# First loads reordered and cut, two more tiles' latents from unscaled tokens, separate PSUM banks for a tile's second transposition

## The chip, the cores and the metric

The kernel runs on one core of one Trainium2 chip. The metric is the device time of one execution in microseconds, the median of several runs; lower is better. Beside the timed runs, one execution was recorded by the hardware profiler, and all views of the profile and the trace come from that one.

## The reference

One encoder layer for 1280 tokens of width 1024 (256 of a prompt, 1024 of a sample), all in float32:

```python
h = rmsnorm(x, attn_norm_g)
proj = h @ w_in                      # 384 q latent | 256 kv latent | 32 rope key | 3 x 512 neighbourhood q, k, v
a = mla_group(proj[..., :o1], proj[..., o1:o2], proj[..., o2:o3], q_norm_g, kv_norm_g, w_uq, w_ukv)
b = na_group(proj[..., o3:], na_rpb)
mix = jnp.concatenate([rmsnorm(a, mla_out_g), rmsnorm(b, na_out_g)], axis=-1)
x = x + mix @ w_o
h2 = rmsnorm(x, ffn_norm_g)
x = x + (jax.nn.silu(h2 @ w_gate) * (h2 @ w_up)) @ w_down
```

with a final `rmsnorm`. For this case only the head of it matters: the norm of the tokens, the first 672 columns of `proj` (the latents), the norms of the q and kv latents with their gains, the rotation of the rope key, and the rope part of the queries, which is computed from the normed q latent. A norm of a token is one scale per row, so `rmsnorm(x) @ w` can be taken as `(x @ w)` scaled per row afterwards.

## The kernel before, in words

The tokens are ten tiles of 128 (`NT`), the width eight chunks of 128 (`KC`). Every float32 product is made of three float32r matmuls (`mm3`, lines 108 to 112): each operand is held as a rounded high part and the remaining low part, and high x high, high x low and low x high accumulate in PSUM. So each operand costs a cast on ScalarE (high) and a subtraction on VectorE or GpSimd (low).

The part up to line 295 computes the latents. Its pieces:

- `load_wc(kc)` (line 138) loads one chunk of the latent weights, 128 x 672, and splits it with the norm's gain folded in (`split_g`). Chunks 0 to 4 land in buffers that later hold other weights, chunks 5 to 7 in a ring of two (`wc_raw`).
- `load_half` and `split_x` (lines 149 to 156) load a half of a transposed token tile and split it into `hT_h` and `hT_l`.
- `rms_x(t)` (line 158) loads the same tokens row by row, squares and sums them on ScalarE and makes the row's scale `r` on GpSimd.
- `scale_x(t)` (line 167) spreads `r` over a matrix on GpSimd (`r_m`), turns it on TensorE (`rr`), multiplies the transposed tile by it on VectorE and splits it again. `hT_h` and `hT_l` hold the scaled tokens from then on, for the q, k and V projections that follow.
- `norm_tile(t)` (line 176) is load, row scale and `scale_x` in one.
- `latents(t, r0)` (line 182) runs 48 matmuls into two accumulators (`lat`, four banks in turns of two: 384 columns for q, 288 for kv and the rope key), copies them out to `c`, norms both latents, rotates the key, and turns `c` on TensorE: four transpositions into one `trc` bank, then two more into the same one bank. With `r0` given, the tokens were not scaled yet and the copy out applies `r0`.
- `rope_q(t)` (line 241) makes the rope part of the queries in the bank `pr` (nine matmuls, a rotation, two transpositions) and stores it to `rope_d`.

Tiles 0 to 2 (`NU = 3`) have their latents taken from unscaled tokens and are scaled afterwards; tile 3 is scaled before the loop, and tiles 4 to 9 by `norm_tile(t + 3)` at the head of turn `t`. In the loop's turn `t` stand, in this order, that norm, `latents(t)`, `scale_x(t)` for the unscaled ones, and `rope_q(t)`.

Behind the loop come the weights of the neighbourhood q and k projection (`qk_weights`, line 300), V's weights and V's matmuls for all tiles (`wv_raw`, `wv_h`, `na_t`), and the q and k projections themselves (`qk_ftile`, line 310, accumulators `pj`). V's weights take the memory that the latent stage's pools (`ra`) free.

Order of the work: all loads go through one queue (SP) in the order in which the program writes them; a load that waits for its buffer holds up those behind it. Stores go through ScalarE's queue. The other engines' instruction orders are written by a planner, which runs the program through a model of times and takes what is ready, earlier lines first; on the chip each engine then follows its list strictly. `HOLD` (line 130) keeps four of the chunks of the q/k projections back until a named step of the latents: `(i, c0)` names weight block `i` and first token `c0`; `(t, 0)`, `(t, 1)` and `(t, 2)` are tile `t`'s first transposition, its second, and the one of its rope queries.

PSUM has eight banks: before the change four for `lat`, one `trc`, one `pr`, two `rr`; when `rr` is freed at turn 7, `pj` takes its two.

Of the kernel before, what the change touches and what calls it, by code (L numbers as in the profile page):

```python
# [39 lines left out]
def encoder_trunk(ctx: ExitStack, tc: tile.TileContext, x_tm, x_T, g_attn, w_c, w_v, w_qk,  # L40
# [97 lines left out]
    def load_wc(kc):  # L138
        nm = ("wqk_raw", "wqk_h", "wqk_l", "wqk_h", "wqk_l")
        raw = (rb.tile([P, KC, P], F32, name=nm[kc], bufs=1 if kc == 0 else 2)  # L140
               .rearrange("p a b -> p (a b)")[:, 0:CW] if kc < 5 else
               rx.tile([P, CW], F32, name="wc_raw", bufs=2))
# [4 lines left out]
        wc.append((h, l))

    def split_x(t, xT, q=None):
        ks = slice(0, KC) if q is None else slice(4 * q, 4 * q + 4)  # L150
# [1 line left out]
        nc.scalar.copy(out=hT_h[sl], in_=xT[:, ks])
        nc.vector.tensor_sub(out=hT_l[sl], in0=xT[:, ks], in1=hT_h[sl])
# [13 lines left out]
    def scale_x(t, xT, r):  # L167
        rm = ra.tile([P, P], F32, name="r_m", bufs=1)
        nc.gpsimd.tensor_scalar(out=rm, in0=ones, scalar1=r, scalar2=1.0, op0=ALU.mult,
                                op1=ALU.mult)  # L170
# [1 line left out]
        nc.tensor.matmul(rr, lhsT=rm, rhs=ident, start=True, stop=True)
# [1145 lines left out]
```

## Time and profile before

| | |
|---|---|
| median of 3 runs | 1643.68 us (1642.41 to 1643.81) |
| the profiled execution, own time | 1647.12 us |
| its span, first to last instruction | 1645.3 us |
| mean granted TensorE clock | 0.991 |
| TensorE busy | 1594.9 us, 97% of the span |
| VectorE busy | 884.6 us, 54% |
| ScalarE busy | 715.5 us, 43% |
| GpSimd busy | 660.4 us, 40% |
| first matmul | 6.68 us after the first instruction |
| first matmul of V | 157.05 us |

A row of the timeline has the start, the duration, the engine, the line, the operation, `out<-in` with the program's names, the shapes, how many were merged, and in brackets how long the engine had been idle before it and what released it. PE is TensorE's matmul, PEld its weight load, DVE VectorE, ACT ScalarE, POOL GpSimd, SP the engine whose queue issues the loads (its rows are marked SPq). Where a helper records an operation, the line is the helper's: L110 to L112 are the three matmuls of `mm3`, L99 and L100 the split of a PSUM bank, L64 every load.

### The profile page before, as it was taken

To read this page: it belongs to the slowest core of one execution; us is meant where nothing else is said; L and a number is where in the kernel's file an instruction comes from. 1 tells how busy PE (TensorE), PEld (TensorE's weight loads), DVE (VectorE), ACT (ScalarE), POOL (GpSimd) and SP (SyncE) were. 2 spreads that over 40 slices of the span, in tenths; PEclk is the share of its full clock that TensorE was granted. 3 is DMA by queue.
4 is the path that set the end of the run, shared out by engine and by line. 5 is a ranking of instruction groups with operands and counts; after the bars stand their busy time and mean duration, and the time that the engine had idled before them with its cause. 6 is when DMAs were issued, how large, how long until landed. Compare 5 with 4: busy or idle time off the path is not lost.

```text
span 1645.3 us, 25695 instructions
## 1 busy us (share of the span) xinstructions
PE 1594.9 (97%) x9601; PEld 1449.9 (88%) x9601; DVE 884.6 (54%) x1473; ACT 715.5 (43%) x1478; POOL 660.4 (40%) x823
## 2 busy tenths in 40 slices
PE   7898999999999999899999999999999999999998
PEld 6897889898888888788889999999999998888886
DVE  4655035455677777534275443344443346876676
ACT  5434145455677777534353222322222333443334
POOL 3461425544111119322686656656656652010002
PEclk9999999999999999999999999999999999999999
DMA  6635312234001013233222322322322337843434
GB/s 220 205 107 147 63 37 54 44 108 159 20 19 34 21 30 100 65 115 135 96 73 94 108 89 60 101 87 95 108 89 65 97 104 256 304 149 96 154 101 152
DMA packets 123244, 171.10 MB, mean 104 GB/s; under 512 B 35504, under 2 KB 67120, under 8 KB 123120
## 3 DMA queue, kind: packets, MB, share of 16 engines
q1 hardware_dynamic: 78880, 120.30, 24.0%
q10 hardware_dynamic: 43680, 46.87, 8.2%
q0 software_dynamic: 560, 2.29, 0.3%
q8 instruction: 75, 1.23, 0.3%
q14 instruction: 49, 0.40, 0.1%
HBM read 118.96 MB, written 50.46 MB: 103 GB/s over the span
## 4 chain that ended last, share of the span: by engine, by line
PE 86%; issue 3%; POOL 3%; DVE 2%; ACT 2%; DMA 2%; SPq 0%; ACTq 0%; POOLq 0%; DVEq 0%
PE M L112 10%; PE M L110 10%; PE M L111 10%; PE d L112 5%; PE d L111 5%; PE d L110 5%; PE o L699 3%; PE tp L689 3%; PE na_o L469 2%; PE po L110 2%; PE po L111 2%; PE po L112 2%; PE pj L110 2%; PE pj L112 2%; PE pj L111 2%
## 5 line engine op out<-in xcount | busy, mean ns | idle before, releaser
L111 PE MATMUL M<-S,wc 128*128 128x320 f32 x1056 | 324.8, 309 | 0.0
L110 PE MATMUL M<-S,wc 128*128 128x320 f32 x1056 | 322.1, 310 | 0.5 <-ACT wc L863 0.2
L112 PE MATMUL M<-S,wc 128*128 128x320 f32 x1056 | 313.1, 310 | 3.9 <-POOL wc L864 3.9
L112 PEld LDWEIGHTS M<-S,wc 128*128 128x128 f32 x1056 | 195.4, 188 | 4.5 <-POOL wc L864 4.5
L110 PEld LDWEIGHTS M<-S,wc 128*128 128x128 f32 x1056 | 197.9, 188 | 1.5 <-ACT wc L863 0.9
L111 PEld LDWEIGHTS M<-S,wc 128*128 128x128 f32 x1056 | 198.6, 188 | 0.0
L864 POOL TENSOR_TENSOR wc<-A,wc 128x512 fp32r<-128x512 f32 x86 | 119.7, 1392 | 84.1 <-ACT wc L863 84.0
L939 DVE TENSOR_TENSOR z<-M,z 128x320 f32<-128x320 f32 x120 | 56.9, 488 | 133.1 <-PE M L112 122.7
L863 ACT CAST wc<-A 128x512 fp32r<-128x512 f32 x86 | 53.5, 622 | 164.7 <-PE M L111 146.7
L864 POOL TENSOR_TENSOR wc<-sum,wc 128x512 fp32r<-128x512 f32 x62 | 87.8, 1417 | 87.0 <-ACT wc L863 87.0
L111 PE MATMUL d<-S,S 128*128 128x512 f32 x310 | 120.6, 390 | 0.0
L112 PE MATMUL d<-S,S 128*128 128x512 f32 x310 | 120.1, 390 | 0.0
L110 PE MATMUL d<-S,S 128*128 128x512 f32 x310 | 119.9, 389 | 0.0
L939 DVE TENSOR_TENSOR zB<-M,zB 128x320 f32<-128x320 f32 x100 | 47.6, 488 | 133.1 <-PE M L112 131.8
L100 DVE TENSOR_TENSOR PT<-tp,PT 128x512 fp32r<-128x512 f32 (+1 forms) x144 | 93.0, 658 | 39.4 <-ACT PT L99 37.9
L863 ACT CAST wc<-sum 128x512 fp32r<-128x512 f32 x62 | 38.4, 619 | 144.3 <-PE M L111 98.1
L99 ACT CAST PT<-tp 128x512 fp32r<-128x512 f32 (+1 forms) x144 | 79.2, 565 | 40.2 <-PE tp L689 37.1
L681 DVE TENSOR_REDUCE mm<-S 128x1 f32<-128x1024 f32 (+1 forms) x80 | 84.8, 1062 | 10.6 <-PE S L112 8.9
L983 ACT CAST S<-as 128x640 fp32r<-128x640 f32 x58 | 42.3, 729 | 96.5 <-issue 58.6
L683 ACT ACTIVATE ex<-S,mm 128x1024 f32<-128x1024 f32 (+1 forms) x80 | 79.7, 996 | 7.5 <-DVE mm L681 6.7
L699 PE MATMUL o<-PT,v 128*128 128x256 f32 x544 | 81.0, 288 | 1.2 <-ACT PT L99 1.2
L689 PE MATMUL tp<-ident,ex 128*128 128x128 f32 x544 | 79.5, 274 | 2.1 <-DVE PT L100 1.2
(401 smaller groups left out, 4054.4 us busy)
## 6 DMA issues: line engine op xcount, KB each, us to landing
as<-act_d SPq DMA_DIRECT2D x73, 320.0 KB
w<-in_w_down_dram SPq DMA_DIRECT2D x44, 256.0 KB
act_d<-z ACTq DMA_DIRECT2D x35, 320.0 KB
act_d<-zB ACTq DMA_DIRECT2D x35, 320.0 KB
A<-in_w_gate_dram SPq DMA_DIRECT2D x42, 256.0 KB
A<-in_w_up_dram SPq DMA_DIRECT2D x42, 256.0 KB
x<-in_x_tm_dram SPq DMA_DIRECT2D x20, 512.0 KB
cT_d<-stg ACTq DMA_DIRECT2D x20, 320.0 KB
```

Of the source, the lines that this page charges most:

```text
L99: i = nc.scalar.copy(out=hi, in_=ps)
L100: nc.vector.tensor_sub(out=lo, in0=ps, in1=hi)
L110: nc.tensor.matmul(out, lhsT=sh, rhs=mh, start=first, stop=False, **kw)
L111: nc.tensor.matmul(out, lhsT=sh, rhs=ml, start=False, stop=False, **kw)
L112: return nc.tensor.matmul(out, lhsT=sl, rhs=mh, start=False, stop=last, **kw).ins
L681: nc.vector.reduce_max(out=nm[:, u:u + 1], in_=S, axis=AX.X, negate=True)
L683: nc.scalar.activation(ex, S, AF.Exp, bias=nm[:, u:u + 1], scale=1.0, accum_out=l[:, u:u + 1])
L689: nc.tensor.transpose(tp[:, j], ex[:, kt * P:(kt + 1) * P], ident)
L699: nc.tensor.matmul(oT, lhsT=vv, rhs=pt[s][g][:, j], start=kt == 0 and s == 0, stop=kt == nkt - 1 and s == 1)
L863: i0 = nc.scalar.copy(out=hi, in_=raw)
L864: i1 = nc.gpsimd.tensor_tensor(out=lo, in0=raw, in1=hi, op=ALU.subtract)
L939: nc.vector.tensor_add(out=o, in0=ps, in1=a)
```

## The change

Five things are edited, all in the latent stage.

1. First loads. The gain vector comes first, then two chunks (a quarter) of tile 0's tokens, weight chunk 0 in two pieces (384 and 288 columns, each split by itself), a quarter of tile 1, weight chunk 1, and the rest of tiles 0 and 1 in quarters and halves between the weight chunks. Tile 2 is loaded in one piece behind the last weight chunk. Weight chunk 7 takes the buffer of chunk 0 instead of the ring.
2. `NU` is 5: tiles 3 and 4 are loaded and split unscaled too, their latents are scaled on the way out, and they are scaled afterwards. The loads of the row tiles, the latents' gains, the cosine and sine tables and the rope weights are put between them in a new order; the rope weights are one load and one split.
3. Tiles 5 to 9 are loaded by `load_tile(t + 5)` in turn `t`, two turns ahead of their `norm_tile(t + 3)`. `r_m` has two buffers, `rr` one bank.
4. A tile's second transposition (`tk`) gets a bank of its own, in the place of the second `rr` bank, for tiles 0 to 6. Tile 9 takes its two transposition banks and its rope bank from the four of `lat`. (`lat` is declared with 512 columns; it filled a bank before as well.)
5. `HOLD` has other steps for three of the four held chunks.

```diff
-    HOLD = {(0, 768): (7, 2), (1, 0): (8, 2), (1, 256): (9, 0), (1, 768): (9, 1)}
-    NU = 3
+    HOLD = {(0, 768): (7, 2), (1, 0): (9, 0), (1, 256): (8, 2), (1, 768): (9, 2)}
+    NU = 5
...
     def load_wc(kc):
-        nm = ("wqk_raw", "wqk_h", "wqk_l", "wqk_h", "wqk_l")
+        nm = {0: "wqk_raw", 1: "wqk_h", 2: "wqk_l", 3: "wqk_h", 4: "wqk_l", 7: "wqk_raw"}.get(kc)
...
-        load(raw, w_c[kc])
         h = ra.tile([P, CW], F32R, name=f"wc_h{kc}")
         l = ra.tile([P, CW], F32R, name=f"wc_l{kc}")
-        split_g(h, l, raw, kc)
+        cuts = (slice(0, QR), slice(QR, CW)) if kc == 0 else (slice(0, CW),)
+        for cs in cuts:
+            load(raw[:, cs], w_c[kc][:, cs])
+        for cs in cuts:
+            split_g(h[:, cs], l[:, cs], raw[:, cs], kc)
...
-    def load_half(t, xT, q):
-        load(xT[:, 4 * q:4 * q + 4], x_T[t, :, 4 * q:4 * q + 4])
-
-    def rms_x(t):
+    def load_part(t, a, b):
+        load(xu[t][:, a:b], x_T[t, :, a:b])
+        split_x(t, xu[t], slice(a, b))
+
+    def load_x(t):
         x = rx.tile([P, D], F32, name="x", bufs=2)
         load(x, x_tm[t * P:(t + 1) * P, :])
+        return x
+
+    def rms_x(x):
...
-        rm = ra.tile([P, P], F32, name="r_m", bufs=1)
+        rm = ra.tile([P, P], F32, name="r_m", bufs=2)
...
-        rr = px.tile([P, P], F32, name="rr", bufs=2)
+        rr = px.tile([P, P], F32, name="rr")
...
-    def norm_tile(t):
-        xT = (rb.tile([P, KC, P], F32, name="wqk_h", bufs=2) if t in (3, 4) else
-              rx.tile([P, KC, P], F32, name="xT", bufs=3))
+    def load_tile(t):
+        xT = rx.tile([P, KC, P], F32, name="xT", bufs=3)
         load(xT, x_T[t])
-        scale_x(t, xT, rms_x(t))
+        return xT, load_x(t)
+
+    def norm_tile(t, xT, x):
+        scale_x(t, xT, rms_x(x))
...
-        tq = pa.tile([P, 4, P], F32, name="trc")
+        last = t == NT - 1
+        tq = pa.tile([P, 4, P], F32, name="lat" if last else "trc", bufs=4 if last else 1)
...
-        tk = pa.tile([P, 4, P], F32, name="trc")
+        tk = (pa if t + 3 >= NT else px).tile([P, 4, P], F32, name="lat" if last else "trc",
+                                              bufs=4 if last else 1)
...
     def load_wr():
-        for c in range(3):
-            raw = rx.tile([P, CW], F32, name="wc_raw", bufs=2)[:, 0:256]
-            load(raw, w_qr[:, c])
-            split_w(wr[:, 0, c], wr[:, 1, c], raw)
+        raw = (rb.tile([P, KC, P], F32, name="wqk_raw").rearrange("p a b -> p (a b)")
+               [:, 0:768].rearrange("p (c n) -> p c n", c=3))
+        load(raw, w_qr)
+        split_w(wr[:, 0], wr[:, 1], raw)
...
-        bank = pa.tile([P, 512], F32, name="pr")
+        last = t == NT - 1
+        bank = pa.tile([P, 512], F32, name="lat" if last else "pr", bufs=4 if last else 1)
...
-    load_half(0, xu[0], 0)
+    xu = [rx.tile([P, KC, P], F32, name="xT", bufs=3) for _ in range(3)]
     load(ga, g_attn)
-    split_x(0, xu[0], 0)
-    halves = [(t, q) for t in range(NU) for q in range(2)][1:]
+    load_part(0, 0, 2)
     for kc in range(KC):
         load_wc(kc)
-        if kc < len(halves):
-            t, q = halves[kc]
-            load_half(t, xu[t], q)
-            split_x(t, xu[t], q)
-    ru = [rms_x(t) for t in range(NU)]
-    norm_tile(NU)
+        for part in {0: ((1, 0, 2),), 1: ((0, 2, 4), (1, 2, 4)), 3: ((0, 4, 8), (1, 4, 8))}.get(kc, ()):
+            load_part(*part)
+    load(xu[2], x_T[2])
+    split_x(2, xu[2])
+    ru = [rms_x(load_x(0))]
     load(gq_b[:, 0:QR], g_q.partition_broadcast(P))
     load(gq_b[:, QR:], g_kv.partition_broadcast(P))
-    load(ck, cos_k)
-    load(sk, sin_k)
-    load_wr()
+    ru.append(rms_x(load_x(1)))
+    for t in (3, 4):
+        xu.append(rb.tile([P, KC, P], F32, name="wqk_h", bufs=2))
+        load(xu[t], x_T[t])
+        split_x(t, xu[t])
+        if t == 3:
+            load(ck, cos_k)
+            load(sk, sin_k)
+            ru.append(rms_x(load_x(2)))
+            load_wr()
+            ru.append(rms_x(load_x(3)))
+    ru.append(rms_x(load_x(4)))
+    ready = {}
     for t in range(NT):
-        if NU < t + 3 < NT:
-            norm_tile(t + 3)
+        if NU <= t + 3 < NT:
+            norm_tile(t + 3, *ready[t + 3])
         stg = latents(t, ru[t] if t < NU else None)
         if t < NU:
             scale_x(t, xu[t], ru[t])
+        if t + 5 < NT:
+            ready[t + 5] = load_tile(t + 5)
```

More of the change, by code (lines that the diff above doesn't have):

```diff
@@ L128, in encoder_trunk @@
     wr = ra.tile([P, 2, 3, 256], F32R, name="wr")
-    wc, step = [], {}
-    HOLD = {(0, 768): (7, 2), (1, 0): (8, 2), (1, 256): (9, 0), (1, 768): (9, 1)}
-    NU = 3
+    wc, step, rrs = [], {}, {}
+    HOLD = {(0, 768): (7, 2), (1, 0): (9, 0), (1, 256): (8, 2), (1, 768): (9, 2)}
+    NU = 5
     def split_g(h, l, raw, kc):
@@ L138, in load_wc, with split_x @@
     def load_wc(kc):
-        nm = ("wqk_raw", "wqk_h", "wqk_l", "wqk_h", "wqk_l")
-        raw = (rb.tile([P, KC, P], F32, name=nm[kc], bufs=1 if kc == 0 else 2)
-               .rearrange("p a b -> p (a b)")[:, 0:CW] if kc < 5 else
+        nm = {0: "wqk_raw", 1: "wqk_h", 2: "wqk_l", 3: "wqk_h", 4: "wqk_l", 7: "wqk_raw"}.get(kc)
+        raw = (rb.tile([P, KC, P], F32, name=nm, bufs=1 if nm == "wqk_raw" else 2)
+               .rearrange("p a b -> p (a b)")[:, 0:CW] if nm else
                rx.tile([P, CW], F32, name="wc_raw", bufs=2))
-        load(raw, w_c[kc])
         h = ra.tile([P, CW], F32R, name=f"wc_h{kc}")
         l = ra.tile([P, CW], F32R, name=f"wc_l{kc}")
-        split_g(h, l, raw, kc)
+        cuts = (slice(0, QR), slice(QR, CW)) if kc == 0 else (slice(0, CW),)
[3 more added lines that the diff above has]
+            split_g(h[:, cs], l[:, cs], raw[:, cs], kc)
         wc.append((h, l))
-    def split_x(t, xT, q=None):
-        ks = slice(0, KC) if q is None else slice(4 * q, 4 * q + 4)
+    def split_x(t, xT, ks=slice(0, KC)):
         sl = (slice(None), ks, slice(t * P, (t + 1) * P))
@@ L167, in scale_x @@
     def scale_x(t, xT, r):
-        rm = ra.tile([P, P], F32, name="r_m", bufs=1)
+        rm = ra.tile([P, P], F32, name="r_m", bufs=2)
         nc.gpsimd.tensor_scalar(out=rm, in0=ones, scalar1=r, scalar2=1.0, op0=ALU.mult,
                                 op1=ALU.mult)
-        rr = px.tile([P, P], F32, name="rr", bufs=2)
-        nc.tensor.matmul(rr, lhsT=rm, rhs=ident, start=True, stop=True)
+        rr = px.tile([P, P], F32, name="rr")
+        rrs[t] = nc.tensor.matmul(rr, lhsT=rm, rhs=ident, start=True, stop=True).ins
         nc.vector.tensor_mul(out=xT, in0=xT, in1=rr.unsqueeze(1).to_broadcast([P, KC, P]))
         split_x(t, xT)
-    def norm_tile(t):
-        xT = (rb.tile([P, KC, P], F32, name="wqk_h", bufs=2) if t in (3, 4) else
-              rx.tile([P, KC, P], F32, name="xT", bufs=3))
+    def load_tile(t):
+        xT = rx.tile([P, KC, P], F32, name="xT", bufs=3)
         load(xT, x_T[t])
-        scale_x(t, xT, rms_x(t))
+        return xT, load_x(t)
+    def norm_tile(t, xT, x):
+        scale_x(t, xT, rms_x(x))
     def latents(t, r0=None):
         ts_ = slice(t * P, (t + 1) * P)
-        pq = pa.tile([P, QR], F32, name="lat", bufs=4)
-        pk = pa.tile([P, QR], F32, name="lat", bufs=4)[:, 0:KVR + RD]
+        pq = pa.tile([P, 512], F32, name="lat", bufs=4)[:, 0:QR]
+        pk = pa.tile([P, 512], F32, name="lat", bufs=4)[:, 0:KVR + RD]
         for kc in range(KC):
```

1 line of the change is left out of this document (removed).

## The prediction

> **What bounds the kernel now.** I read the profile's page first: the span, the engines, the granted clock, the chain that ended last.
>
> ```profile
> span 1645.3 us, 25695 instructions
> PE 1594.9 (97%) x9601; PEld 1449.9 (88%) x9601; DVE 884.6 (54%) x1473; ACT 715.5 (43%) x1478; POOL 660.4 (40%) x823
> PE 86%; issue 3%; POOL 3%; DVE 2%; ACT 2%; DMA 2%; SPq 0%; ACTq 0%; POOLq 0%; DVEq 0%
> ```
>
> TensorE is the bound nearly everywhere, so a change that adds and removes almost no matmuls can only win or lose where TensorE stands still or runs slowly. Everything the diff touches lies ahead of the V projection, so next I cut that part at TensorE's gaps. Columns: stretch, its length, then busy time of PE, PEld, DVE, ACT, POOL, the granted clock, the DMA share and GB/s.
>
> ```profile
> 0.00:6.67 6.67, 0.00 (x0) 0.00 (x0) 0.88 (x4) 2.75 (x3) 0.68 (x6) 1.00 0.65 174
> 6.67:24.00 17.33, 16.79 (x96) 16.04 (x96) 10.84 (x14) 11.37 (x17) 1.10 (x4) 1.00 0.71 254
> 24.00:31.00 7.00, 7.00 (x44) 6.79 (x44) 0.56 (x2) 4.17 (x10) 2.40 (x7) 1.00 0.94 301
> 31.00:42.00 11.00, 6.70 (x30) 5.15 (x30) 7.83 (x11) 5.25 (x14) 9.94 (x25) 0.84 0.46 151
> 42.00:50.90 8.90, 8.90 (x65) 8.76 (x63) 6.56 (x11) 2.20 (x5) 3.89 (x7) 1.00 0.63 189
> 50.90:62.00 11.10, 7.66 (x32) 6.94 (x31) 8.80 (x15) 6.83 (x13) 6.09 (x12) 0.69 0.46 153
> 62.00:75.80 13.80, 13.80 (x97) 13.79 (x97) 5.36 (x10) 6.39 (x13) 3.81 (x11) 1.00 0.72 219
> 75.80:100.00 24.20, 21.60 (x152) 20.90 (x151) 16.64 (x25) 9.40 (x24) 19.52 (x24) 1.00 0.48 145
> 100.00:124.00 24.00, 24.00 (x158) 22.91 (x157) 9.49 (x26) 7.68 (x24) 8.81 (x25) 1.00 0.41 109
> 124.00:157.05 33.05, 28.04 (x157) 22.95 (x156) 15.54 (x37) 13.77 (x34) 6.77 (x21) 1.00 0.51 143
> 157.05:190.00 32.95, 32.62 (x140) 26.19 (x141) 6.16 (x9) 8.26 (x14) 10.13 (x6) 1.00 0.40 96
> ```
>
> Length minus PE is idle time; where the clock stands below 1.00, busy time times (1 - clock) is also lost. Start: 6.67 us. To 24: 0.54. From 31 to 42: 4.30 idle + 6.70 x 0.16 = 5.4. From 50.9 to 62: 3.44 + 7.66 x 0.31 = 5.8. From 75.8 to 100: 2.6. Tail before V: 5.0. Together 26.0 us: the whole field of this change. After 157 TensorE is nearly full (32.62 of 32.95), so what is won before it should reach the end. Who ended the gaps is in the table of TensorE's waits up to 165 us (total, times, longest):
>
> ```profile
> PE lat L110 <- ACT wc_h L134: 6.7, 1, 6.7
> PE rr L172 <- POOL r_m L169: 4.0, 4, 1.5
> PE pr L260 <- POOL qr L257: 2.5, 3, 0.9
> PE lat L110 <- ACT hT_h L152: 2.3, 1, 2.3
> PE pr L111 <- POOL wr L96: 1.8, 2, 1.4
> PE na_t L110 <- ACT wv_h L134: 1.5, 1, 1.5
> PE trc L226 <- DVE stg L100: 1.0, 2, 0.7
> ```
>
> The first is the wait for the first weights. `r_m` and `hT_h` are the norm of a tile that must be scaled before its latents; `wr` the split rope weights; `qr` and `stg` the hand-overs inside a tile's tail; `wv_h` V's first weights.
>
> **First loads.** The first transfers and what waited for them:
>
> ```profile
> 0.72 0.39 SPq L64 DMA_DIRECT2D xT<-in_x_T_dram  x1
> 1.64 0.42 SPq L64 DMA_DIRECT2D wqk_raw<-in_w_c_dram  x1
> 3.54 0.62 ACT L152 CAST hT_h<-xT 128x512 fp32r<-128x512 f32 x1 [1.54 <-DMA xT<-in_x_T_dram]
> 5.77 0.85 ACT L134 ACTIVATE wc_h<-wqk_raw,ga 128x672 fp32r<-128x672 f32 x1 [1.61 <-DMA wqk_raw<-in_w_c_dram]
> 6.68 0.93 PE L110 MATMUL lat<-wc_h,hT_h 128*128 128x384 f32 x2 [6.68 <-ACT wc_h L134]
> ```
>
> Half a tile (256 KB) was usable 2.8 us after its issue; the 336 KB of weights behind it 2.23 us later, 151 KB per us. The new order puts 128 KB of tokens and 192 KB of weights first: 272 KB less, 1.8 us by that rate. The q part's split takes 384/672 of 0.85, 0.49 us, 0.36 less. That makes 2.2 us at most. At the other end, the first weights' issue stays near 1.64 us, and if 2.8 us is a floor per transfer they come at 4.4, matmuls near 5.0: 1.7 us won. But extra issues (some 0.45 us each) lie in front of later chunks, and if those starve TensorE the start can lose 0.5. I take -1.4 (range -2.2 to +0.5): the first chunk feeds twelve matmuls, six each of tiles 0 and 1, so the rest stays covered. [...]
>
> Weight chunk 7 goes to another buffer. In the table of the load queue's waits that is
>
> ```profile
> SPq L64 <- DMA wc_raw<-in_w_c_dram: 5.2, 1, 5.2
> SPq L64 <- DMA rope_d<-sr: 62.0, 5, 50.3
> ```
>
> the 5.2. TensorE hid it behind two tiles' matmuls (96 instructions in the stretch to 24), so it counts nothing by itself; it frees the queue for the token rows whose square sums scale the latents. That release is needed 1.4 us earlier now; I leave the 0.54 us of idle time in the stretch to 24 as it is.
>
> **Two more tiles from unscaled tokens.** Tile 3's path to its matmuls in the timeline, and the wait for tile 4's:
>
> ```profile
> 30.08 1.06 ACT L162 ACTIVATE x<-x 128x1024 f32<-128x1024 f32 x1 [1.02 <-DMA x<-in_x_tm_dram]
> 33.85 0.36 POOL L169 TENSOR_SCALAR r_m<-ones,rx 128x128 f32<-128x128 f32 x1
> 34.27 0.49 PE L172 MATMUL rr<-ident,r_m 128*128 128x128 f32 x2 [1.34 <-POOL r_m L169]
> 36.05 1.05 ACT L152 CAST hT_h<-wqk_h 128x1024 fp32r<-128x1024 f32 x1 [3.07 <-DVE wqk_h L173]
> 40.35 1.22 DVE L153 TENSOR_TENSOR hT_l<-wqk_h,hT_h 128x1024 fp32r<-128x1024 f32 x1
> 53.45 0.45 PE L110 MATMUL lat<-wc_h,hT_h 128*128 128x384 f32 x1 [2.30 <-ACT hT_h L152]
> ```
>
> Now tile 3 needs only its load, one cast and one subtraction (1.05 + 1.22). Bytes ahead of it: eight weight chunks 2.75 MB, three tiles 1.57, two row tiles 1.05, gains 0.33, itself 0.52, together 6.2 MB. 174 GB/s x 6.67 us brings 1.16; the other 5.0 MB at 254 GB/s take 20 us: landed at 26.5, split by 29. TensorE reaches it near 31.5 (tile 2's 48 matmuls at 7.00/44 = 0.16 us are 7.6 us, from 24 less 1.4, plus transpositions), so 2.5 us of slack. Tile 4 has 2.4 MB more ahead of it, 8 us at 301 GB/s, split by 37, needed near 41. Tile 5, the first to be scaled ahead, is wanted only after 48; its load waits for tile 0's rescaled split, near 26. So the chain above leaves TensorE's path, and with it the clock's fall to 0.84 and 0.69: 11.2 us are open. What remains: the rope weights, now one load and two POOL instructions behind a third row tile; at the rates used here they land near 31, and tile 3 now covers them.
>
> The cost: each of the two tiles is split twice.
>
> ```profile
> L152 ACT CAST hT_h<-wqk_h 128x1024 fp32r<-128x1024 f32 x2 | 2.1, 1037 | 3.1 <-DVE wqk_h L173 3.1
> L153 DVE TENSOR_TENSOR hT_l<-wqk_h,hT_h 128x1024 fp32r<-128x1024 f32 x2 | 2.4, 1222 | 2.3 <-ACT hT_h L152 2.3
> L173 DVE TENSOR_TENSOR wqk_h<-wqk_h,rr 128x1024 f32<-128x1024 f32 x2 | 2.4, 1217 | 1.1 <-PE rr L172 1.1
> ```
>
> That is 2.1 us of ACT and 2.4 of DVE, beside matmuls if DVE has room. From 24 to 62 DVE works 0.56 + 7.83 + 6.56 + 8.80 = 23.75 us; the same TensorE work without gaps takes 38 - 11.2 = 26.8, and DVE then has 26.2 to do in it: 98%. It is late next. It can lean on the stretches beside (5.36 of 13.80 from 62 on, and 6.5 us idle before 24), so I count 8 of the 11.2 as won (0 to 11.2; below 0 in the rival).
>
> **Earlier loads of tiles 5 to 9, a second `r_m`.** Rows and columns of a tile are requested two turns ahead of the norm, not with it. The gap from 75.8 to 100 (2.6 us) holds a 1.5 us wait for `r_m`; q and k weights, loaded behind tile 9 on the same queue, come earlier, and their first chunks can fill TensorE. One `rr` bank in place of two adds a wait of at most one scaling (1.22 us) to a tile with spare time. I take -1.6 (-2.6 to +1.2).
>
> **Tail.** The second transposition of a tile no longer waits for the first to be copied out: 1.0 us in the waits. Tile 9 gets accumulation banks, and the four held q/k chunks are released in another order, the last one only behind tile 9's rope transposition. That keeps some 5.5 us of matmuls (24 of 512 columns, at 32.62/140 = 0.23 as in V's stretch) for the wait for V's weights, whose loads stand behind stores of `rope_d` (62.0 in the queue's waits); but it withholds them while `qr` is made. Of 5.0 I take -1.5 (-4 to +3).
>
> **The sum** for the profiled execution, 1647.1 us with a span of 1645.3: -1.4 - 8 - 1.6 - 1.5 = -12.5, plus 1 for a planner's order that the chip does not follow exactly (the gap ahead of `wv_h` is such a one: 0 to 4): -11.5, so 1635.6. The runs' median is 1643.7, 3.4 below that execution; the same difference gives 1632.2.
>
> **The rivals.** *Half of it.* The middle closes only in part, because DVE's 98% hands 5 us back as late evacuations: -3.5 to -7, near 1638.5. For it: DVE's sum. Against: the neighbouring stretches have room. *Nothing.* TensorE reaches the tail earlier but waits there for V's weights: their loads come only behind tile 9's stores, and if tile 9's chain does not move, -11.5 turns into about -1, 1642.7. Against: that chain hangs on tile 9's latents, which TensorE itself sets. *Slower.* With tiles 5 to 7 loaded early, DVE also does their scaling and split (2.44 each, 7.3 us) before the evacuations that free the accumulators: 33.5 us of DVE work in 26.8 of TensorE's. TensorE then waits 6.7 us in many short gaps, and as the stretch from 50.9 to 62 shows, that is when the clock falls; half speed over 20 us of it costs another 10. Sum: -11.2 - 1.4 + 6.7 + 10 = +4, 1648. It decides once DVE is over 100% from 24 to 62. [...]
>
> **Chances.** Most of it (5.5 to 18 us won) 0.62, half of it 0.16, nothing 0.08, slower 0.14. A measurement here tells about 0.2%, 3.3 us. Faster by more: 0.62 and most of the half, 0.76. Within: 0.10. Slower: 0.14. The likeliest case alone spans 1626 to 1638; with the half case, nothing, and the tail's and start's upper ends the range is 1625 to 1646.
>
> **What would show it.** First matmul near 5.2 us; chunk 7's split no longer waiting for its load; 96 latent matmuls done by 22. From 24 to 62 clock 1.00 and PE idle below 3 us; no wait of a latent matmul for `hT_h`. V's first matmul near 145 in place of 157. Wrong: DVE at 95% or more with waits on `c` copies (half or slower), a clock of 0.5 anywhere between 24 and 62, a gap above 3 us ahead of V (nothing), a first matmul after 6.2 us.

## The result and the profile after

| | before | after |
|---|---|---|
| median of 5 runs each | 1643.2 us (1642.41 to 1643.81) | 1631.41 us (1629.95 to 1634.1) |
| ratio, 95% interval | | 0.9935 (0.9923 to 0.9947) |
| the profiled execution: own time, span | 1647.12, 1645.3 | 1629.95, 1628.2 |
| first matmul, first matmul of V | 6.68, 157.05 | 5.32, 145.88 |

The change makes the kernel 0.65% faster, 11.8 us by the medians. The forecast was 1632.2 us, range 1625 to 1646. The two profiled executions lie 17.1 us apart, and 11.2 of that is there at V's first matmul. The rest comes behind the edited part: before's profile has a stretch at half clock from 378.8 to 385.6 us that after's lacks, and one near 690 us is 6.8 us long where after's is 3.4. So I compare times by medians, and the two traces up to V.

The page's head, engines and chain of the kernel after:

```profile
span 1628.2 us, 25717 instructions
PE 1586.7 (97%) x9601; PEld 1444.8 (89%) x9601; DVE 887.0 (54%) x1477; ACT 716.5 (44%) x1482; POOL 662.9 (41%) x819
PE 86%; issue 3%; POOL 3%; DMA 3%; ACT 2%; DVE 2%; ACTq 0%; SPq 0%; POOLq 0%; DVEq 0%
```

TensorE is still the bound and has the same 9601 matmuls. The stretches ahead of V, with the columns that the prediction names (length, then PE, PEld, DVE, ACT, POOL, clock, DMA, GB/s):

```profile
0.00:5.32 5.32, 0.00 (x0) 0.00 (x0) 0.61 (x4) 2.35 (x4) 0.69 (x6) 1.00 0.52 131
5.32:24.00 18.68, 18.68 (x105) 18.48 (x106) 12.23 (x17) 13.65 (x23) 2.22 (x7) 1.00 0.99 366
24.00:31.00 7.00, 7.00 (x51) 6.99 (x50) 5.16 (x7) 5.20 (x14) 6.51 (x14) 1.00 0.64 231
31.00:42.00 11.00, 9.93 (x68) 9.33 (x68) 5.74 (x8) 7.32 (x17) 9.93 (x20) 1.00 0.76 247
42.00:50.90 8.90, 8.90 (x64) 8.85 (x63) 8.43 (x16) 5.34 (x13) 5.68 (x13) 1.00 0.57 154
50.90:62.00 11.10, 10.66 (x75) 10.03 (x73) 9.04 (x16) 6.21 (x15) 5.88 (x14) 1.00 0.99 308
62.00:69.00 7.00, 6.77 (x46) 6.53 (x47) 4.89 (x9) 4.64 (x12) 3.68 (x5) 1.00 0.68 218
69.00:92.00 23.00, 18.24 (x126) 17.15 (x125) 15.69 (x23) 8.06 (x19) 18.09 (x30) 1.00 0.36 107
92.00:114.00 22.00, 22.00 (x150) 21.05 (x149) 9.05 (x24) 6.67 (x21) 5.47 (x17) 1.00 0.33 87
114.00:145.90 31.90, 28.75 (x145) 23.94 (x144) 14.70 (x35) 12.42 (x27) 4.71 (x12) 0.89 0.51 141
```

Losses counted as in the prediction: 5.32 at the start and nothing up to 31 (before 6.67 and 0.54). From 31 to 62 they are 1.07 + 0.44 = 1.5 (before 11.2). From 62 to 69 it is 0.23. From 69 to 92, 4.76 (before 2.6 from 75.8 to 100). In the tail, 3.15 idle and 28.75 x 0.11 = 3.2 from the clock, 6.3 together (before 5.0). In all 18.1 in place of 26.0, which is 7.9 of the 11.2 us by which V begins earlier.

One loss is in neither sum. The traces hold no clock record ahead of 10.13 us (before) and 10.55 us (after), and a stretch without a record reads 1.00. But the 384-column matmuls follow each other every 0.32 us up to there and every 0.17 us behind it, so both kernels start at half clock, before for 3.5 us and after for 5.2, which costs 1.7 and 2.6. The 96th latent matmul ends at 22.78 us in place of 23.49: 0.7 us earlier, half of the first matmul's lead.

The rest of the 11.2 is busy time; the stretch up to V in the trace of before, and then of after:

```profile
0.00:157.05 157.05, 134.49 (x818) 124.21 (x818) 82.48 (x148) 69.80 (x153) 63.02 (x138) 0.97 0.56 169
```

```profile
0.00:145.88 145.88, 130.91 (x815) 122.34 (x815) 85.53 (x154) 71.85 (x158) 62.86 (x132) 0.98 0.59 185
```

TensorE was busy 3.6 us less for nearly the same records, with about the same recorded loss to the clock (1.07 + 2.37 before, 3.2 after); which matmuls became shorter I have not followed further. TensorE's longest waits of after up to 160 us:

```profile
PE lat L110 <- ACT wc_h L134: 5.3, 1, 5.3
PE pr L271 <- POOL qr L268: 3.2, 2, 1.8
PE lat L110 <- ACT stg L99: 2.2, 1, 2.2
PE trc L232 <- DVE c L224: 1.6, 1, 1.6
PE pr L110 <- DVE sr L105: 1.4, 2, 0.9
```

No latent matmul waits for a scaled tile's `hT_h` any more. What is left stands in the hand-overs of a tile's own end: `qr`, `c`, `stg`, `sr`.

### The profile page after: what moved, and what is told of

Read it like the earlier page. It is cut to its first block, busy times and chain, and to the rows that moved or that the text cites. A ratio compares the mean times of both kernels' runs of the same rounds, so it can differ in the third digit from the quotient of the medians.

```text
span 1628.2 us, 25717 instructions
## 1 busy us (share of the span) xinstructions
PE 1586.7 (97%) x9601; PEld 1444.8 (89%) x9601; DVE 887.0 (54%) x1477; ACT 716.5 (44%) x1482; POOL 662.9 (41%) x819
## 4 chain that ended last, share of the span: by engine, by line
PE 86%; issue 3%; POOL 3%; DMA 3%; ACT 2%; DVE 2%; ACTq 0%; SPq 0%; POOLq 0%; DVEq 0%
PE M L112 10%; PE M L110 10%; PE M L111 10%; PE d L112 5%; PE d L111 5%; PE d L110 5%; PE o L719 3%; PE tp L709 3%; PE po L110 2%; PE pj L110 2%; PE pj L111 2%; PE pj L112 2%; PE po L111 2%; PE po L112 2%; PE na_o L489 2%
## 5 line engine op out<-in xcount | busy, mean ns | idle before, releaser
L732 POOL TENSOR_TENSOR ob<-ob 128x128 f32<-128x128 f32 x40 | 18.3, 457 | 156.1 <-ACT ob L729 152.5
```

## The experiments

Each kernel was measured side by side with before, whose median was then 1642.2 to 1644.06 us, and the ratio is to that. Effects are compared by these ratios, where the text doesn't name the medians.

### Each part undone

**Two tiles fewer from unscaled tokens.** Tiles 3 and 4 keep their new places in the load queue, but are scaled ahead of their latents.

```diff
-    NU = 5
+    NU = 3
...
-        split_x(t, xu[t])
...
-            ru.append(rms_x(load_x(3)))
-    ru.append(rms_x(load_x(4)))
-    ready = {}
+            ready = {3: (xu[3], load_x(3))}
+    ready[4] = (xu[4], load_x(4))
```

> The changed kernel with only the number of unscaled tiles put back to 3; tiles 3 and 4 keep their new early loads but are scaled before their latents. Theory A (the gain is the middle: TensorE no longer waits for the norm of tiles 3 and 4): 7 to 9.5 us of the gain go, about 1640; latent matmuls wait for hT_h or hT_l between 31 and 62 us, the clock falls to 0.5 there, V's first matmul moves from 146 to about 154. Rival B (the earlier loads of rows, gains and tiles alone bring the norms in time): about 1632, no clock fall in that stretch.

Measured: 1623.72 us, ratio 0.9891 (0.9876 to 0.9907). Both expectations missed on the same side. Undoing the edit that was credited with the middle's 8 us makes the kernel 7.7 us faster still by the medians, 7.2 by the ratios. Stretches of this kernel:

```profile
24.00:31.00 7.00, 6.34 (x45) 6.08 (x43) 3.43 (x6) 3.69 (x10) 6.60 (x13) 1.00 0.70 243
31.00:42.00 11.00, 8.56 (x40) 7.31 (x41) 9.46 (x16) 6.69 (x15) 7.12 (x18) 0.77 0.47 128
42.00:51.00 9.00, 9.00 (x60) 8.99 (x60) 6.06 (x11) 3.87 (x9) 1.74 (x5) 0.91 0.64 198
...
69.00:92.00 23.00, 22.71 (x159) 22.38 (x158) 16.61 (x29) 12.15 (x32) 18.22 (x28) 1.00 0.60 181
...
114.00:146.00 32.00, 32.00 (x168) 27.07 (x167) 16.47 (x32) 15.95 (x32) 3.28 (x10) 1.00 0.63 165
```

The middle does open again: 0.66 + 2.44 + 8.56 x 0.23 + 9.00 x 0.09 = 5.9 us from 24 to 51. But from 69 to 92 only 0.3 is lost in place of 4.8, and the tail is full, 32.00 of 32.00. V begins at 137.8, 8.1 earlier.

**The first loads.** The old order and sizes, chunk 7 back in the ring.

```diff
-        nm = {0: "wqk_raw", 1: "wqk_h", 2: "wqk_l", 3: "wqk_h", 4: "wqk_l", 7: "wqk_raw"}.get(kc)
+        nm = {0: "wqk_raw", 1: "wqk_h", 2: "wqk_l", 3: "wqk_h", 4: "wqk_l"}.get(kc)
...
-        cuts = (slice(0, QR), slice(QR, CW)) if kc == 0 else (slice(0, CW),)
+        cuts = (slice(0, CW),)
...
-    load_part(0, 0, 2)
+    split_x(0, xu[0], slice(0, 4))
+    halves = [(t, q) for t in range(3) for q in range(2)][1:]
...
+        if kc < len(halves):
+            t, q = halves[kc]
+            load_part(t, 4 * q, 4 * q + 4)
```

> The changed kernel with the first loads as before: tile halves, weight chunk 0 in one piece, chunk 7 in the ring. Theory A: only the start comes back, first matmul 6.7 instead of 5.3 and the idle 0.5 before 24, so 1.5 to 2 us, about 1633.3. Rival C (the start carries more: the queue blocked behind chunk 7 delays the token rows and with them every later release): the gaps between 24 and 62 grow too, 5 us or more, 1636 to 1639.

Measured: 1636.39 us, ratio 0.9964 (0.995 to 0.9977), as the expectation of the larger loss had it. By the ratios the new first loads are worth 0.0029 of the time, 4.8 us, more than the 1.4 that the first matmul moves: the wait for `wc_h` is 7.1 (before 6.7), chunk 7 is in the ring again (a wait of 5.2 us before, 1.0 after), and from 5 to 24 us the DMA moves 274 GB/s in place of 361, so everything behind it comes later too: from 24 to 62 3.6 us are lost in place of 1.5. In its waits new ones stand for the evacuation (`trc` for `stg` 2.8, `lat` for `c` 1.6).

**The banks.** One `trc` bank for both transpositions of every tile, two for `rr`.

```diff
-        rr = px.tile([P, P], F32, name="rr")
+        rr = px.tile([P, P], F32, name="rr", bufs=2)
...
-        tk = (pa if t + 3 >= NT else px).tile([P, 4, P], F32, name="lat" if last else "trc",
-                                              bufs=4 if last else 1)
+        tk = pa.tile([P, 4, P], F32, name="trc")
...
-        bank = pa.tile([P, 512], F32, name="lat" if last else "pr", bufs=4 if last else 1)
+        bank = pa.tile([P, 512], F32, name="pr")
```

> The changed kernel with the PSUM banks as before: both transpositions in one trc bank, rope bank pr for all tiles, rr two banks. Theory A: the wait of the second transposition returns, 1 us, and the tail of tile 9 shifts by at most 2: 1631 to 1634. Rival D (the banks carry the gain of the tail): V's first matmul 4 us or more later, 1635 or more.

Measured: 1637.52 us, ratio 0.9968 (0.9957 to 0.9979). The rival holds, with V's first matmul at 149.9, 4.0 later: in this kernel the banks are worth 0.0033, 5.4 us. The first row of TensorE's waits in that kernel:

```profile
PE trc L235 <- DVE stg L100: 5.7, 4, 2.8
```

Before, that wait was 1.0. With the other gaps closed, a second transposition that waits for the first to be copied out is no longer hidden.

**The earlier loads of tiles 5 to 9.** Back in the turn of the norm, one `r_m`.

```diff
-        rm = ra.tile([P, P], F32, name="r_m", bufs=2)
+        rm = ra.tile([P, P], F32, name="r_m", bufs=1)
...
-            norm_tile(t + 3, *ready[t + 3])
+            norm_tile(t + 3, *load_tile(t + 3))
...
-        if t + 5 < NT:
-            ready[t + 5] = load_tile(t + 5)
```

> The changed kernel without the loads two turns ahead: tiles 5 to 9 are loaded in the turn of their norm, r_m has one buffer. Theory A: the loads were not late for tiles 5 to 9, so 0 to 1 us lost; and since the q/k weights come later again, GpSimd's work on them no longer falls between 65 and 88 us, and the 4.8 us idle in the stretch from 69 to 92 shrinks: 1628 to 1632. Rival E (the loads ahead are what keeps TensorE fed from tile 5 on): tile 5's latents wait, clock falls near 50 to 62 us, 1635 to 1640.

Measured: 1629.66 us, ratio 0.9929 (0.9912 to 0.9946). That is within the interval of the change as a whole: the earlier loads are worth nothing that can be measured. One expectation missed: the q and k weights do not come later again. GpSimd's first multiplication on them, after the change and in this kernel:

```profile
65.54 1.90 POOL L325 TENSOR_TENSOR wqk_raw<-wqk_raw,ga 128x1024 f32<-128x1024 f32 x1 [3.05 <-DMA wqk_raw<-in_w_qk_dram]
65.78 1.90 POOL L323 TENSOR_TENSOR wqk_raw<-wqk_raw,ga 128x1024 f32<-128x1024 f32 x1 [5.76 <-DMA rope_d<-sr]
```

The queue issues the loads of tiles 7, 8 and 9 at 47.3, 52.2 and 57.7 us after the change and at 46.7, 51.9 and 56.8 here, so asking for them earlier in the program did not bring them earlier.

**The releases of the held chunks.** The old `HOLD`.

```diff
-    HOLD = {(0, 768): (7, 2), (1, 0): (9, 0), (1, 256): (8, 2), (1, 768): (9, 2)}
+    HOLD = {(0, 768): (7, 2), (1, 0): (8, 2), (1, 256): (9, 0), (1, 768): (9, 1)}
```

> The changed kernel with the releases of the four held q/k chunks as before: (1,0) behind tile 8's last transposition, (1,256) behind tile 9's first, (1,768) behind tile 9's second, so that no chunk is kept back until tile 9's rope transposition. Prediction's step 'Tail': keeping one chunk back leaves matmuls for the wait for V's weights, so without it the idle time from 114 us to V's first matmul grows by 1 to 3 us and the time is 1633 to 1635. Rival: after tile 9's rope transposition nothing is waited for any more that a chunk could fill (in the changed kernel the one long wait of the tail, 2.2 us, lies ahead of a latent matmul at 120.8), so the order of the releases only moves gaps: 1630 to 1632.5, and V's first matmul within 1.5 us of the changed kernel's 145.9.

Measured: 1633.6 us, ratio 0.994 (0.9924 to 0.9957), no difference from the change that can be measured. V's first matmul is at 144.9 and the idle time of the tail 3.2, as with the new releases, which is the rival's reading. The time is not: all four runs (1632.85 to 1635.59) lie above its 1632.5, and the median lies in the range of the prediction's step. But that step's own sign, 1 to 3 us more of idle time in the tail, did not come.

The five effects do not add up: 4.8 + 5.4 - 7.2 - 1.0 + 0.8 = 2.8 by the ratios, of 10.7. What no run here undoes is the place of tiles 3 and 4 and of the rope weights in the load queue, and parts that need each other count in each undoing differently. Each edit also makes the planner write another order, which no undoing keeps apart from the edit itself. Where the other 8 us belong is open.

### The unscaled tiles alone

Before's kernel, with tiles 3 and 4 unscaled and nothing else.

```diff
-    NU = 3
+    NU = 5
...
-    norm_tile(NU)
+    for t in (3, 4):
+        xu.append(rb.tile([P, KC, P], F32, name="wqk_h", bufs=2))
+        load(xu[t], x_T[t])
+        split_x(t, xu[t])
+        ru.append(rms_x(t))
...
```

> The kernel before with only tiles 3 and 4 taken unscaled (first loads, loads of tiles 5 to 9, banks and holds as before). If the five unscaled tiles are a gain by themselves: the stretch from 31 to 62 us loses its 9.6 us and the total falls to 1633 to 1637. If they only shift the wait (theory F): the middle gap shrinks, but gaps or a lag of the rope chain appear behind it and the total stays between 1639 and 1646.

Measured: 1645.87 us, ratio 1.0025 (1.0016 to 1.0033): a little slower than before. The gap only moved. Stretches of this kernel:

```profile
31.00:42.00 11.00, 10.10 (x67) 9.51 (x66) 5.86 (x8) 4.83 (x11) 9.93 (x21) 1.00 0.35 114
...
51.00:62.00 11.00, 9.57 (x64) 9.01 (x64) 9.03 (x16) 6.23 (x13) 6.01 (x14) 1.00 0.68 187
62.00:69.00 7.00, 4.76 (x31) 4.10 (x30) 7.00 (x9) 3.95 (x8) 3.27 (x6) 0.85 0.89 315
69.00:92.00 23.00, 19.68 (x111) 19.10 (x110) 16.32 (x23) 8.87 (x22) 19.22 (x26) 0.82 0.39 123
```

The mechanism works as described: 0.9 us of idle time from 31 to 42 where before lost 5.4. It is given back from 62 to 92: 2.24 + 4.76 x 0.15 + 3.32 + 19.68 x 0.18 = 9.8 us, where before lost 2.35. VectorE is busy 7.00 of 7.00 from 62 to 69. V's first matmul is at 156.9, before's was at 157.05. About 1 us of this profile is not the edit's: the first matmul is at 7.02 and full pace comes only at 12.29 us (14 matmuls in the 3.42 us ahead of it, 23 in the 3.41 behind; before's has 24 in 3.42 us from 10.09 on), so the 96th latent matmul already ends 1.1 us later than before's. And up to V the waits of a second transposition for `stg`, 1.0 us before, are 4.5 here: the single `trc` bank, which the whole change replaces, takes part of the gain too.

### Where the two tiles give it back

The theory after these runs: rescaling and splitting tiles 3 and 4 a second time, and GpSimd's work on the first two blocks of q and k weights, which now begins at 65.5 us in place of 84.4, stand in the strict lists of VectorE and GpSimd ahead of the small steps of a tile's end (`rc`, `c`, `qr`, `stg`). So the rope matmuls of the tiles lag, and the last of them come when nothing else is left to run. What brings that work forward is the unscaled tiles: with 3 of them it begins at 78.1, with 4 at 74.9, with 5 at 65.5, and in before's kernel with 5 at 72.1. One such place in the trace of after, two of GpSimd's steps on the second block, the `qr` behind them, and TensorE:

```profile
79.65 1.90 POOL L325 TENSOR_TENSOR wqk_raw<-wqk_raw,ga 128x1024 f32<-128x1024 f32 x1 [2.21 <-DMA wqk_raw<-in_w_qk_dram]
82.26 1.04 POOL L94 TENSOR_SCALAR wqk_h<-wqk_raw 128x1024 fp32r<-128x1024 f32 x1
84.16 0.72 POOL L268 TENSOR_TENSOR qr<-qr,qr 128x256 f32<-128x256 f32 x1
84.93 0.44 PE L271 MATMUL pr<-ident,qr 128*128 128x128 f32 x2 [1.75 <-POOL qr L268]
```

VectorE had made the inputs of that `qr` by 80.02. GpSimd kept to its list there: it stood idle for 2.21 us, to 79.65, until the block had landed, and `kr_t`, which stands behind that block in its list and whose `c` VectorE had copied by 78.16, came at 81.50.

The rope matmuls (three of each kind per tile) from 100 to 150 us and V's first, after, with 3 unscaled tiles, and with the GpSimd work held (next experiment), as groups by line. After:

```profile
L110 PE MATMUL pr<-wr,stg x12: 276/278/390, 101.1 to 129.2; 128*128 128x256 f32 x12
L110 PE MATMUL na_t<-wv_h,hT_h x23: 388/392/397, 145.9 to 161.5; 128*128 128x512 f32 x23
```

With 3 unscaled tiles:

```profile
L110 PE MATMUL pr<-wr,stg x6: 280/281/281, 107.9 to 122.2; 128*128 128x256 f32 x6
L110 PE MATMUL na_t<-wv_h,hT_h x34: 388/394/397, 137.8 to 161.7; 128*128 128x512 f32 x34
```

With GpSimd's work held:

```profile
L110 PE MATMUL pr<-wr,stg x9: 276/281/383, 108.7 to 125.1; 128*128 128x256 f32 x9
L110 PE MATMUL na_t<-wv_h,hT_h x29: 388/392/397, 141.8 to 161.5; 128*128 128x512 f32 x29
```

Besides tile 9, whose rope matmuls write a bank of `lat` and are not in these groups, four tiles' rope matmuls stand behind 100 us after the change, two with 3 unscaled tiles, three with the work held; V's start follows, 145.9, 137.8, 141.8. The link is loose: without the earlier loads it is four tiles too, and V starts at 142.2.

**Four unscaled tiles.**

```diff
-    NU = 5
+    NU = 4
...
-        split_x(t, xu[t])
+        if t < NU:
+            split_x(t, xu[t])
...
```

> The changed kernel with four unscaled tiles instead of five (3 gave 1623.7, 5 gave 1631.4). Theory F (the extra split and later scaling of an unscaled tile load VectorE while GpSimd gets the q/k weights early, the rope chain falls behind, and the lag comes back as idle time from 69 to 92 us and in the tail): between the two in its lag, but the middle gap of 3 closed: rope matmuls of tile 4 begin near 80 us (91 with five, 76 with three), 1620 to 1627. Theory G (no trend, each version has its own order): anything from 1622 to 1636 with no link between that lag and the gaps.

Measured: 1627.35 us, ratio 0.9902 (0.9888 to 0.9916), V at 140.9: between 3 (0.9891) and 5 (0.9935), just above the expected 1620 to 1627. The lag is between them too: tile 4's rope matmuls begin at 83.3 (75.6 with three, 91.0 with five). The intervals of 5 and 4 do not overlap; 4 and 3 can't be told apart. So the trend that theory F asks for rests on the step from 4 to 5, and theory G, that each order has its own luck, is not excluded by it.

**GpSimd's weight work held back.** With 5 unscaled tiles, the three GpSimd instructions on each of the first two q/k weight blocks are issued only behind the rope additions of tiles 4 and 5.

```diff
-        nc.gpsimd.tensor_tensor(out=t1, in0=t1, in1=t2, op=ALU.add)
+        step[t, 3] = nc.gpsimd.tensor_tensor(out=t1, in0=t1, in1=t2, op=ALU.add).ins
...
+        with ExitStack() as es:
+            if i < 2:
+                es.enter_context(tc.issue_after(step[4 + i, 3]))
+            nc.gpsimd.tensor_tensor(out=raw, in0=raw, op=ALU.mult,
+                                    in1=ga.unsqueeze(2).to_broadcast([P, KC, P]))
+            split_w(wh, wl, raw)
```

> The changed kernel with GpSimd's three instructions on each of the first two q/k weight blocks held behind the rope addition of tiles 4 and 5; nothing else moves. If GpSimd's early weight work is what delays the rope chain (one half of theory F): the 4.8 us idle between 69 and 92 fall below 1.5, the tail's gap at 118 us and its half clock go too, V's first matmul at 139 or earlier, about 1622 to 1625. If VectorE is the cause (the other half): the gap only moves or shrinks by a third, 1628 to 1632, and the weights come late for their first use near 105 us.

Measured: 1627.88 us, ratio 0.9905 (0.9889 to 0.992), just clear of the interval of the change. Stretches of this kernel:

```profile
62.00:69.00 7.00, 5.42 (x38) 5.13 (x36) 4.77 (x10) 4.02 (x10) 3.58 (x9) 1.00 0.68 212
69.00:92.00 23.00, 22.52 (x147) 22.44 (x148) 15.90 (x30) 8.99 (x22) 9.86 (x21) 0.93 0.39 106
```

The idle time from 69 to 92 falls from 4.76 to 0.48 when GpSimd does 9.86 us there in place of 18.09. So that gap comes from where GpSimd's weight work stands, which is shown. Not all of it is won: 1.58 us of idle time stand in the stretch ahead (after: 0.23) and 22.52 x 0.07 = 1.6 go to the clock, so from 62 to 92 3.6 us are lost in place of 5.0. By the medians the kernel is 3.5 us faster than the change. The other signs missed: V begins at 141.8 and not by 139, and the tail still has 3.4 us of half clock. The time lies at the edge of the second expectation's range and 2.9 us above the first's, so holding this work back takes away only part of the lag.

**VectorE's rescaling held back.** The scaling of tiles 3 and 4 is written in turns 5 and 6.

```diff
-        r = ra.tile([P, 1], F32, name="rx", bufs=4)
+        r = ra.tile([P, 1], F32, name="rx", bufs=8)
...
-        if t < NU:
+        if t < 3:
             scale_x(t, xu[t], ru[t])
+        if t in (5, 6):
+            scale_x(t - 2, xu[t - 2], ru[t - 2])
```

> The changed kernel with the scaling of tiles 3 and 4 (multiply, cast, subtraction: 3 x 2 instructions, 2.4 us of VectorE each) written two turns later, in turns 5 and 6; their latents stay unscaled. If VectorE's load between 40 and 75 us is the cause: rope matmuls of tile 4 before 80 us, gap from 69 to 92 below 1.5 us, tail without its gap, 1620 to 1625. It also makes GpSimd's weight work later, since the weights' buffers are the two tiles' own; the trace shows by how much. If neither engine is the cause: 1629 to 1633.

Measured: 1631.04 us, ratio 0.992 (0.9906 to 0.9934). V begins at 140.6, 5.3 earlier than after, and yet the time is the same. Ahead of V it loses 21.15 x 0.07 = 1.5 us to the clock where after loses 3.2; yet the mean granted clock of its profiled execution is 0.993 where after's is 0.995, so by my estimate more of it is lost behind V, at a place that is not shown. What it wins ahead of V is not in the medians. The idle time from 69 to 92 falls to 1.85, where below 1.5 was expected, and tile 4's rope matmuls begin at 89.2, not before 80. The time is that of the second expectation. VectorE's share of the lag is not shown by it.

**Both:** four unscaled tiles and GpSimd's work held.

```diff
-    NU = 5
+    NU = 4
...
+                es.enter_context(tc.issue_after(step[4 + i, 3]))
...
```

> The changed kernel with four unscaled tiles and GpSimd's work on the first two q/k weight blocks held behind the rope additions of tiles 4 and 5. With four tiles alone 1627.4, with the hold on five tiles 4.1 us earlier at V. If both loads (VectorE's and GpSimd's) add up in the lag: gaps between 62 and 92 us below 1 us, V's first matmul at 138 or earlier, 1621 to 1624. If they are the same loss: 1626 to 1628.

Measured: 1625.29 us, ratio 0.9899 (0.9885 to 0.9914): between the two expectations, and no different from either part alone. V begins at 137.8, as the first expectation has it, but from 62 to 92 2.1 us are idle, not below 1.

**One more chunk to fill with.** In the change, the first held chunk is released a tile earlier.

```diff
-    HOLD = {(0, 768): (7, 2), (1, 0): (9, 0), (1, 256): (8, 2), (1, 768): (9, 2)}
+    HOLD = {(0, 768): (6, 2), (1, 0): (9, 0), (1, 256): (8, 2), (1, 768): (9, 2)}
```

> The changed kernel with only the first held chunk released one tile earlier, with tile 6's rope transposition instead of tile 7's. If the tail's gap (2.2 us idle at 118 us and 6.8 us of half clock behind it) is a lack of released matmuls: gap and half clock go, V's first matmul near 141, 1626 to 1628. If the lag alone decides: 1630 to 1632, the gap elsewhere in the tail.

Measured: 1631.45 us, ratio 0.9927 (0.9915 to 0.994). The 2.2 us wait of the tail is gone from its waits, but those for `qr` rise from 3.2 to 5.1. Matmuls to fill with are not what the tail lacks; the gap stands where the late step is.

**A faster start on the best version.** With 3 unscaled tiles, the row tiles 2 and 3 are loaded ahead of the tables and rope weights, and five matmuls on constants, whose result nothing reads, run while the first loads are under way.

```diff
-    NU = 5
+    NU = 3
...
+    warm = px.tile([P, P], F32, name="rr")
+    for _ in range(5):
+        nc.tensor.matmul(warm, lhsT=ident, rhs=ones, start=True, stop=True)
...
+            ru.append(rms_x(load_x(2)))
+            ready = {3: (xu[3], load_x(3))}
...
```

> The changed kernel with three unscaled tiles (1623.7 by itself), plus two things that touch different places: the row tiles 2 and 3 are loaded ahead of the tables and rope weights, and five matmuls on constants, whose result nobody reads, run on TensorE before the first weights land. Expected of the first: tile 3's norm comes 2 us earlier, the idle and half-clock loss between 31 and 51 us (5.3 us with three tiles) falls below 3. Expected of the second: full clock from about 7 us instead of 10.5, 96 latent matmuls done 1.5 us earlier. Together 1619 to 1622; if the order of rows is not what tile 3 waits for, 1622 to 1624.

Measured: 1633.75 us, ratio 0.9954 (0.9941 to 0.9968), 10 us slower than the version that it was to improve. Both expectations missed. The stretches from 31 to 42 and from 51 to 62 lose 3.93 + 7.07 x 0.16 + 2.79 + 8.21 x 0.16 = 9.2 us, against 5.9 from 24 to 51 and nothing from 51 to 62 in that version, and V begins at 145.3 in place of 137.8. In its waits stand the rope weights (`pr` for `wr`, 1.8) and `qr` (3.6). As two things were edited at once, it doesn't say which of them did it.

## Why the prediction was right, and where it was wrong

The total was right, 1632.2 against 1631.4, and the sign. That it came out so close is luck, for the terms were not. One by one:

- **First loads, -1.4.** The first matmul is right: 5.32 against 6.68, -1.36, and the 0.54 of idle time to 24 is gone too. Of that, only 0.7 is left at the 96th matmul, in the main because the half clock at the start, which the prediction's table reads as 1.00, lasted 5.2 us in place of 3.5. But the term left a larger part out: undone, these edits cost 4.8 us. The prediction priced the load of chunk 7 out of the ring at nothing because TensorE hid it then, adding that it "frees the queue". The queue's waits for the ring (`wc_raw`) fall from 5.2 to 1.0 us, and up to 24 us the DMA moves 366 GB/s in place of 254. How much of the 4.8 is chunk 7's and how much the new order's, no run shows, as both were undone together.
- **Two more tiles from unscaled tokens, -8.** The size of the middle's gain is right (11.2 to 1.5, so 9.7), and its credit is the failed step. "I count 8 of the 11.2 as won" took an emptied gap for time won at the end. Alone, the edit closes the gap and gives the time back, most of it from 62 to 92 (1.0025); taken out of the change, it makes the kernel 7.2 us faster by the ratios. The prediction named VectorE as "late next" and put the danger into the stretch from 24 to 62, as a sum of busy time over TensorE's. There VectorE had room: 5.16 + 5.74 + 8.43 = 19.33 of the 26.9 us from 24 to 50.9, 72%, not 98%, since the second scaling came only at 58 us (tile 3) and 70 us (tile 4). From 69 to 92, where the time was lost, no engine was full as a whole (VectorE 15.69 and GpSimd 18.09 of 23.00), though in turn each was for some 3.4 us (rows at 82.20 and 85.70 in the last section). With 3 unscaled tiles GpSimd is busy for 18.22 us in the same stretch and TensorE loses 0.3. What counted was which instruction stood ahead of which.
- **Earlier loads and a second `r_m`, -1.6.** Wrong. The stretch got worse, 2.6 to 4.8, where the prediction expected the early q/k weights to fill TensorE. The weights did come earlier, and GpSimd's work on them is what opened the gap, as holding it back shows. But it was not this edit that brought them: without it they come as early, and with 3 unscaled tiles they come 12.5 us later. Undoing the earlier loads changes nothing that can be measured.
- **Tail, -1.5.** Wrong by 2.8: 5.0 became 6.3. Half of it is clock. The banks, priced at the 1.0 us of their wait before, are worth 5.4 in the changed kernel: a wait that stands behind others is sized by what it would be once those are gone.
- **The planner's +1** can't be told apart from these.

Of the rivals, *Half* named VectorE, whose part in the lag is open, and a wrong place; its sum, near 1638.5, did not come. *Slower* had a chain like the one found, scaling ahead of the evacuations with a falling clock behind it; the kernel with the unscaled tiles alone shows such a loss, 9.8 us from 62 to 92, which there eats most of the gain. *Nothing* did not come: V's weights were not waited for. So the sum came out right because unscaled tiles priced too high met first loads and banks priced too low.

Of the signs that were named: the first matmul (5.2 foreseen, 5.32), chunk 7's split no longer waiting for its load, no wait for `hT_h`, the clock 1.00 and 1.5 us idle from 24 to 62, V at 145 (145.88) all came; the 96 latent matmuls done by 22 came late, at 22.78. The signs did not test the credit: V at 145 would have looked the same whichever edit had won the time.

The best version here is the change with 3 unscaled tiles: 1623.72 us, 0.9891 of before, and below the changed kernel's 1631.41 with no overlap of the intervals.

Open: how the 8 us left over in the undoings are shared; VectorE's part in the lag; how much of it is the planner's order of each kernel; why the tail's 2.2 us wait for tile 9's `stg` is as long as it is, and which of the two edits of the last kernel made it slow.

## What to carry to other kernels

When a gap is closed by moving work to other engines, follow the moved work to where it now stands in those engines' lists and ask which small step waits behind it; a sum of busy time over a stretch does not show that. Change a composite in parts, once by undoing and once alone: here the part with the clearest gain in its own stretch was the one that cost time at the end. A weight preparation that comes earlier than it is needed is not free where its engine also carries a chain: with GpSimd's held back, the idle time from 69 to 92 fell from 4.76 to 0.48 us.
